# A two-layer hybrid trunk on one core: memory projected behind the second norm, stick breaking with queries and keys first, loads of constants and input moved

## The chip, the core and the metric

The kernel runs on one core of a Trainium2 chip. TensorE (PE) multiplies matrices, VectorE (DVE) and ScalarE (ACT) do elementwise work, GpSimd (POOL) only clears a few tiles, and SyncE (SP) issues every load and store. The metric is the device time of one execution in microseconds (us), lower is better. Before the change it is 1094.56 us, the median of 3 runs (1094.49 to 1095.02).

## The reference

The input is a sequence of 256 vectors of width 1024, in float32, with a fixed memory of 256 vectors. There are two layers; layer 0 mixes with an RWKV-7 recurrence, layer 1 with stick-breaking attention. Each layer is three residual blocks, each with a layer norm behind it:

```python
for i in range(DEPTH):                                   # DEPTH = 2
    x = layer_norm(ALPHA * x + 0.5 * swiglu(x, ffn1_w_gate[i], ffn1_w_up[i], ffn1_w_down[i]), ...)
    if i % 2 == 0:
        proj = x @ rwkv_w_in[0]                          # 2560 mixer columns, 256 memory queries
        mix = rwkv7_mix(proj[..., :RWKV_SHIFT], ...)
    else:
        proj = x @ sb_w_in[0]                            # q, k, v of 768 columns, 256 memory queries
        mix = stick_breaking_mix(...)
    heads = concatenate([mix, memory_attention(mq, mem_k, mem_v)], axis=-1)
    x = layer_norm(ALPHA * x + heads @ w_out[i], ...)
    x = layer_norm(ALPHA * x + 0.5 * swiglu(x, ffn2_w_gate[i], ffn2_w_up[i], ffn2_w_down[i]), ...)
```

The memory's keys and values, `mem @ w_mem_kv`, are computed once and used in both layers. The feed-forward width is 2816. In stick breaking the weight of a key is `exp(log_sigmoid(z) + later)`, where `later` is the sum of `-softplus(z)` over the keys between it and the query, so a softplus and a running sum stand between scores and output.

## The kernel before

The sequence is split into two halves of 128 rows, `hf` 0 and 1, each with its residual rows `xs[hf]` and their transpose `xT[hf]`. A float32 product with weights is made of three products of rounded parts (`mm3`, line 666): every weight piece of 512 KB is loaded to a `raw` tile, ScalarE rounds it to a `hi` tile, and VectorE subtracts to get the `lo` tile (`piece`, line 638). There are 10 raw, 9 hi and 9 lo buffers. A feed-forward network runs in 11 blocks of 256 columns (`ffn_block`, line 776): 8 steps of gate and up products into one bank of PSUM (tag `gu`), the activation, a transpose, and the down products into two accumulator banks of the half (`acc0` or `acc1`). A block listed in `WHOLE` (line 60) makes its down products in plain float32 from the raw weights, without hi and lo tiles. FFN intermediates sit in two buffers of tag `ta`, which other small tiles share.

The program lists operations in the order of the lines from 1448 on. For each layer it runs the first FFN with half 0 ahead of half 1, then `norm(0, ...)`; then the mixer of half 0, with the remaining FFN blocks of half 1 spread between its steps (`alternate`, line 1419); then `norm(1, ...)`; then the mixer of half 1 is opened, `mixed_out(0, ...)` multiplies half 0's heads with `w_out`, `norm(0, ...)` follows, and the second FFN's blocks of half 0 are spread between the steps of half 1's mixer. The dictionaries `RW` and `SB` (lines 50 and 51) say how many FFN steps go behind each named step of a mixer (`yield "nat"` and so on). `PRE[i]` is the number of steps of half 1's mixer that are listed before `mixed_out(0)`.

In layer 0 `memory_kv` (line 844) stands between `norm(0)` with one block of half 1 and the mixer of half 0. It loads the memory's rows, transposes them, multiplies them with four pieces of `w_mem_kv` and leaves `memKT` and `memV`. `mem_attention` (line 868) computes scores, softmax and values with them and writes the last two of the eight transposed pieces of the heads into `xT[hf]`; both mixers call it inside their own steps, with the accumulator banks of their half. `mixed_out` (line 1404) takes the four pieces of `w_out` in the order 3, 0, 1, 2; piece 3 belongs to the memory heads.

`stick` (line 1319) projects five times 512 columns: the last 256 columns of V with the memory queries, then q, q with k, k, the first 512 columns of V; then it does the memory attention, then the scores, softplus, running sums and outputs.

The listed order is not the order of issue. `Plan` (line 133) records all operations with their dependences and a price for each. `Plan.order` (line 348) then schedules them as a list scheduler with one clock for each engine; `Plan.latest` (line 499) computes from a schedule how late each operation may start; `Plan.improve` (line 544) makes 24 such schedules, with priorities from the latest starts, shaken at random from `SEED`, and keeps the one whose planned end is first. Loads go through SP's one queue in an order of their own (`nc.in_turn("load", ...)`): they are sorted by planned latest start, those in `lead` by the latest start of a named operation less 4 us. An SP load whose buffer is not free yet holds up all loads behind it.

Of the kernel before, what the change touches and what calls it, by code (L numbers as in the profile page):

```python
# [47 lines left out]
FIRST = 2  # L48
PRE = (0, 3)
RW = dict(p0=0, p1=0, p2=0, p3=0, p4=0, lb=0, sub=14, rb=0.5, kq=1, nat=0.5, dy=4, dt=2, c0=1.0, c1=1, c2=1.5, c3=2, t0=0, t1=10)  # L50
SB = dict(z0=3.0, z1=0, ln=2.0, e0=1.0, e1=1.5, o=6.0)
HOLD = (2, 4)
# [6 lines left out]
BESIDE = (True, False)  # L59
WHOLE = (((0, 1, 2, 3, 4, 5, 6, 8, 9, 10), (0, 1, 2, 4, 5, 6, 7, 8, 9)), ((), ()))  # L60


LINE = 16
BLK = 16
_LEVELS = [16, 32]
# [62 lines left out]
PATIENCE = 8  # L128
SEED = 144
TURN = 47040.0  # L130
# [474 lines left out]
def kernel(ctx, tc, const, x, mem, f1g, f1u, f1d, f2g, f2u, f2d, ln_g, ln_b, w_out, w_mem_kv,  # L605
# [168 lines left out]


    def ffn_block(w, c, halves, beside, whole):
        gv, uv, dv = (m.rearrange("(k p) c -> p k c", p=P) for m in w)
# [37 lines left out]
        o = {hf: ps("gu") for hf in halves}  # L815
        for k in range(KT):
            wh, wl = (t[:, k % 2] for t in gu[k // 2])
            for hf in halves:
                mm3(o[hf], xT[hf][0][:, k], xT[hf][1][:, k], wh, wl, k == 0, k == KT - 1)
            yield  # L820
        hs = {}
# [45 lines left out]

    def mem_attention(hf, mqT):

        rs = new(tp_, [P, 3, NMH], F32, "rs", "rs", 2)  # L870
        banks = [ps(f"acc{hf}").rearrange("p (j m) -> p j m", j=2) for p in range(2)]
        rows = [slice(p * HD, (p + 1) * HD) for p in range(2)]
# [5 lines left out]
        for p, scv in enumerate(banks):  # L878
# [16 lines left out]
            nc.copy(turned_e[-1], pt.rearrange("p (j m t) -> p j m t", j=2, m=2))  # L895
        o = ps(f"acc{hf}")
        ov = o[:, :MEMW].rearrange("p (j t) -> p j t", j=2)
# [7 lines left out]

    def sl(n, shape=None):
        return new(mp, shape or [P, MIX], F32, n, n)

# [16 lines left out]
    R = {}  # L925

    def rwkv_constants():
        vrow = new(tp_, [44, P], F32, "ta", "vrow", 2)
        for r0, n, src in ((0, 20, r_mu), (20, 6, r_a0), (26, 6, r_kk), (32, 6, r_ka)):
            nc.in_turn("load", nc.sync.dma_start(vrow[r0:r0 + n], src[0].rearrange("(a b) -> a b", b=P)))  # L930
        nc.in_turn("load", nc.sync.dma_start(vrow[38:44], r_rk[0].rearrange("(a c) b -> a (c b)", c=2)))
        gup = new(cp, [P, MIX], F32, "gup", "gup")
        nc.in_turn("load", nc.sync.dma_start(gup, r_gup[0]))
        vc = cp.tile([P, 44], F32, tag="vc", name="vc")
        pt = ps("tp")
        nc.tensor.transpose(pt[:, :44], vrow, ident[:44, :44])
        nc.copy(vc, pt[:, :44])
        for n, a, b in (("mu", 0, 20), ("a0", 20, 26), ("k_k", 26, 32), ("k_a", 32, 38), ("r_k", 38, 44)):
            R[n] = vc[:, a:b]
        rkb = cp.tile([P, NT, NH], F32, tag="rkb", name="rkb")  # L940
        nc.vector.tensor_tensor(rkb, hsel, bc(R["r_k"], 2, [P, NT, NH]), ALU.mult)
        S = new(cp, [P, NT, 2, HD], F32, "S", "S")
        nc.gpsimd.memset(S, 0.0)
        lastc = cp.tile([P, 20], F32, tag="lastc", name="lastc")
        nc.gpsimd.memset(lastc, 0.0)
        R.update(gup=gup, rkb=rkb, S=S, lastc=lastc)

    def rwkv(hf, res):
# [123 lines left out]
        shifted(1792, 512, lambda i: zv[:, 2 + i])  # L1072
        mem_attention(hf, mq)

# [244 lines left out]
    def stick(hf, res):  # L1319
# [7 lines left out]
        B[hf] = kT, V  # L1327
        t = project(hf, sb_in[0], 2048, 512)
        nc.copy(V[:, 512:768], t[:, 0:256])
        mq = new(mp, [P, 2, P], F32, "mq", "mq")  # L1330
        nc.copy(mq, turned(t, 2, 2), 0.125)
        yield "p"
        t = project(hf, sb_in[0], 0, 512)
# [9 lines left out]
        yield "p"  # L1343
        t = project(hf, sb_in[0], 1536, 512)
        nc.copy(V[:, 0:512], t)
        yield "p"
        mem_attention(hf, mq)
        zs, sps, first, logs = {}, {}, [], []
        v3 = lambda t: t.rearrange("q (i t) -> q i t", i=3)
        for si, ts in enumerate(range(hf, -1, -1)):  # L1350
            zm = zs[ts] = sl("qr" if si == 0 else "Sk", [P, 4, 384])
            sps[ts] = [sl(n, [P, 2, 384]) for n in (("L", "Lm") if si == 0 else ("T", "Tt"))]
            for jg in range(2):
# [15 lines left out]
                first.append(nc.scalar.activation(e, e, AF.Exp, scale=-1.0).i)  # L1369
                yield "z1"  # L1370
        for ts in zs:
            for jg in range(2):
                e, zz = sps[ts][jg], zs[ts][:, 2 * jg:2 * jg + 2]
                logs.append(nc.scalar.activation(e, e, AF.Ln, bias=1.0))
                logs[-1].after += first
                nc.vector.scalar_tensor_tensor(e, zz, 0.0, e, ALU.max, ALU.add)
            yield "ln"
        for ts in zs:
            for g in range(4):
                zm = zs[ts][:, g]  # L1380
                cu = ps("tp")
                nc.tensor.matmul(cu[:, :384], K_("tri"), sps[ts][g // 2][:, g % 2], start=True, stop=ts == hf)
                if ts != hf:
                    nc.tensor.matmul(cu[:, :384], K_("ones"), sps[hf][g // 2][:, g % 2], start=False, stop=True)
                nc.vector.tensor_sub(zm, zm, cu[:, :384])
                nc.scalar.activation(zm, zm, AF.Exp).after += [o.i for o in logs]
                yield "e0"
                yield "e1"
        tss = sorted(zs)
        for g in range(2):  # L1390
            o = ps(ac)
# [11 lines left out]

    def mixed_out(hf, y, w):
        t = xT[hf]
        if y is not None:
            to_T(y, t, 0, NT)
        open_acc(hf)
        for n in range(2):
            yield from cols_mm(acc[hf][n], t, cols_pieces(w, n * 512, 512, (3, 0, 1, 2)))  # L1410

# [104 lines left out]
```

## Time and profile before

| | us |
|---|---|
| median of 3 runs | 1094.56 |
| the profiled execution | 1096.41 |
| its span, first to last instruction | 1094.4 |
| TensorE busy | 1067.0 |
| VectorE busy | 895.0 |
| ScalarE busy | 719.9 |
| mean granted TensorE clock | 0.993 |

The span is what the trace covers; the profiled execution has some 2 us around it, and it is one run, slower than the median by 1.85 us. A line of the kernel says little here, because nearly all operations are recorded by one helper (line 601); tiles tell more. `xTh` and `xTl` are the transposed rows, `hi_`, `lo_` and `raw_` weights, `ps_29r` and `ps_30r` the two banks of `gu`, `ps_25r` to `ps_28r` the accumulators, `ps_2r` and `ps_3r` the banks for transposes and small products. The buffer of a tile keeps the name of its first user, so `h_31r` may hold constants, and `qr_404r` and `L_370r` hold scores and softplus in layer 1. A busy TensorE means that records of matmuls follow on one another; their ends are modelled.

### The profile page before, as it was taken

Reading aid. Unit: us, or ns where it says so; the run is one execution under the profiler, and the core shown is the slowest. Engines: PE = TensorE matmul, PEld = TensorE weight load, DVE = VectorE, ACT = ScalarE, POOL = GpSimd, SP = SyncE. Lnnn points to the kernel's source line nnn. Section 1 sums busy time; section 2 is a strip of 40 time slices with the busy share of each in tenths; the row PEclk is TensorE's granted clock in tenths of the full one; section 3 lists DMA queues with packets and bytes.
Section 4 is the critical chain, followed back from the end, with each engine's and each line's share of the span. In section 5 each row is a group of like instructions: output and inputs, shape, how many; then the busy total and the mean of one; then the engine's idle time right before and its main releaser. Section 6 shows DMA issues by size and latency. Waiting matters only on the chain.

```text
span 1094.4 us, 17466 instructions
## 1 busy us (share of the span) xinstructions
PE 1067.0 (97%) x6217; PEld 852.9 (78%) x6217; DVE 895.0 (82%) x1269; ACT 719.9 (66%) x991; POOL 2.7 (0%) x14
## 2 busy tenths in 40 slices
PE   7999999999799999999999999999989999999996
PEld 6878887877688777778888888888867777888885
DVE  6577676999999998787779965659799989987777
ACT  6466556966379684556657654538896899766652
POOL 0000000000000000000000000000000000000000
PEclk9999999999899999999999999999999999999999
DMA  9499768775778698699789976758978987999881
GB/s 335 160 356 386 255 221 286 260 246 193 247 230 285 232 295 274 210 329 336 254 273 365 307 262 204 229 159 287 382 270 293 340 301 239 396 358 316 249 292 59
DMA packets 209784, 300.13 MB, mean 274 GB/s; under 512 B 13684, under 2 KB 157216, under 8 KB 209698
## 3 DMA queue, kind: packets, MB, share of 16 engines
q1 hardware_dynamic: 209698, 299.03, 80.7%
q8 instruction: 48, 0.79, 0.3%
q14 instruction: 38, 0.31, 0.1%
HBM read 297.93 MB, written 1.05 MB: 273 GB/s over the span
## 4 chain that ended last, share of the span: by engine, by line
PE 90%; DVE 6%; DMA 2%; issue 1%; ACT 1%; SPq 0%; DVEq 0%; ACTq 0%
PE ps_30r L601 27%; PE ps_29r L601 27%; PE ps_28r L601 8%; PE ps_27r L601 8%; PE ps_25r L601 7%; PE ps_26r L601 7%; PE ps_2r L601 3%; PE ps_3r L601 3%; DVE x L601 1%; DMA raw_45r<-in_sb_w_in_dram 1%; DMA raw_21r<-in_ffn_w_up_dram 1%; DMA raw_9r<-in_ffn_w_up_dram 1%; DVE lb_475r L601 0%; DVE lo_8r L601 0%; DVE S_110r L601 0%
## 5 line engine op out<-in xcount | busy, mean ns | idle before, releaser
L601 ACT ACTIVATE h_31r<-ps_30r 128x256 f32<-128x256 f32 (+1 forms) x53 | 22.8, 430 | 33.6 <-PE ps_30r L601 33.6
L601 ACT ACTIVATE h_32r<-ps_29r 128x256 f32<-128x256 f32 (+1 forms) x53 | 22.0, 414 | 30.0 <-PE ps_29r L601 29.6
L601 PE MATMUL ps_29r<-hi_37r,xTh 128*128 128x512 f32 x58 | 24.2, 417 | 0.0
L601 PE MATMUL ps_29r<-hi_37r,xTl 128*128 128x512 f32 x58 | 22.7, 392 | 0.0
L601 PE MATMUL ps_29r<-lo_38r,xTh 128*128 128x512 f32 x58 | 22.6, 390 | 0.0
L601 PE MATMUL ps_30r<-hi_16r,xTh 128*128 128x512 f32 x54 | 22.6, 418 | 0.0
L601 PE MATMUL ps_29r<-hi_22r,xTh 128*128 128x512 f32 (+1 forms) x54 | 21.9, 406 | 0.0
L601 PE MATMUL ps_30r<-hi_10r,xTh 128*128 128x512 f32 x54 | 21.9, 405 | 0.0
L601 PE MATMUL ps_30r<-hi_40r,xTh 128*128 128x512 f32 x52 | 21.8, 420 | 0.0
L601 DVE TENSOR_TENSOR h_32r<-h_32r,ps_29r 128x256 f32<-128x256 f32 x32 | 13.4, 418 | 9.6 <-ACT h_32r L601 9.2
L601 PE MATMUL ps_30r<-hi_7r,xTh 128*128 128x512 f32 x50 | 21.2, 424 | 0.0
L601 PE MATMUL ps_30r<-hi_16r,xTl 128*128 128x512 f32 x54 | 21.2, 392 | 0.0
L601 PE MATMUL ps_30r<-lo_17r,xTh 128*128 128x512 f32 x54 | 21.1, 392 | 0.0
L601 PE MATMUL ps_30r<-lo_11r,xTh 128*128 128x512 f32 x54 | 21.1, 391 | 0.0
L601 PE MATMUL ps_30r<-hi_10r,xTl 128*128 128x512 f32 x54 | 21.1, 391 | 0.0
L601 PE MATMUL ps_29r<-lo_23r,xTh 128*128 128x512 f32 (+1 forms) x54 | 20.3, 376 | 0.8 <-DVE lo_23r L601 0.8
L601 PE MATMUL ps_29r<-hi_7r,xTh 128*128 128x512 f32 x50 | 20.9, 418 | 0.0
L601 PE MATMUL ps_30r<-hi_19r,xTh 128*128 128x512 f32 x50 | 20.8, 417 | 0.0
L601 PE MATMUL ps_30r<-hi_13r,xTh 128*128 128x512 f32 x50 | 20.6, 413 | 0.0
L601 PE MATMUL ps_29r<-lo_8r,xTh 128*128 128x512 f32 x50 | 20.2, 404 | 0.5 <-DVE lo_8r L601 0.5
L601 PE MATMUL ps_29r<-hi_10r,xTh 128*128 128x512 f32 x50 | 20.6, 411 | 0.0
L601 PE MATMUL ps_2r<-cst,x 128*128 128x128 f32 x48 | 8.8, 313 | 12.0 <-DVE x L601 6.5
(1909 smaller groups left out, 3958.0 us busy)
## 6 DMA issues: line engine op xcount, KB each, us to landing
raw_9r<-in_ffn_w_gate_dram SPq DMA_DIRECT2D x32, 256.0 KB, 5.4
raw_9r<-in_ffn_w_up_dram SPq DMA_DIRECT2D x32, 256.0 KB, 5.0
raw_18r<-in_ffn_w_down_dram SPq DMA_DIRECT2D x16, 512.0 KB, 4.8
raw_12r<-in_ffn_w_gate_dram SPq DMA_DIRECT2D x31, 256.0 KB, 5.8
raw_12r<-in_ffn_w_up_dram SPq DMA_DIRECT2D x31, 256.0 KB, 4.7
raw_24r<-in_ffn_w_down_dram SPq DMA_DIRECT2D x15, 512.0 KB, 6.1
raw_39r<-in_ffn_w_down_dram SPq DMA_DIRECT2D x15, 512.0 KB, 5.9
raw_42r<-in_ffn_w_down_dram SPq DMA_DIRECT2D x15, 512.0 KB, 6.0
```

The lines of the kernel that those rows point to most:

```text
L601: fn(*[at(x) for x in a], **{n: at(x) for n, x in k.items()})
```

## The change

1. `memory_kv` is taken from before half 0's mixer in layer 0 to behind `norm(1, ...)`. The mixer of half 0 in layer 0 no longer calls `mem_attention`; it hands its memory queries on, and the attention runs behind `memory_kv` with banks of tag `gu`. `mixed_out(0)` of layer 0 takes the pieces of `w_out` in the order 0, 1, 2, 3.
2. `stick` projects q and k first. V and the memory queries are projected behind the scores, and the memory attention follows them.
3. The constants' loads get a fixed early place in SP's queue. The second half's input is loaded and transposed in the first FFN block that needs it, whose gate and up products go half by half; each half's input is loaded in two pieces.
4. Numbers of the plan: `PRE`, `RW`, `SB`, `WHOLE` and `SEED`. Names that are new and switched off (`PARTED` empty, `LATE` false) change nothing.

```diff
-PRE = (0, 3)
-RW = dict(p0=0, p1=0, p2=0, p3=0, p4=0, lb=0, sub=14, rb=0.5, kq=1, nat=0.5, dy=4, dt=2, c0=1.0, c1=1, c2=1.5, c3=2, t0=0, t1=10)
-SB = dict(z0=3.0, z1=0, ln=2.0, e0=1.0, e1=1.5, o=6.0)
+PRE = (0, 0)
+RW = dict(p0=0, p1=0, p2=0, p3=0, p4=0.5, lb=0, sub=14, rb=0.5, kq=1, nat=10, dy=4, dt=1.5, c0=1.0, c1=1, c2=6, c3=2, t0=0, t1=10)
+SB = dict(z0=3.0, z1=0, ln=2.0, e0=1.0, e1=1.5, o=12)
-WHOLE = (((0, 1, 2, 3, 4, 5, 6, 8, 9, 10), (0, 1, 2, 4, 5, 6, 7, 8, 9)), ((), ()))
+WHOLE = (((0, 1, 2, 3, 4, 5, 6, 8, 9, 10), (0, 1, 2, 4, 5, 6, 7, 9)), ((3,), ()))
+MEMTAG = 'gu'
+PARTED = ()
+LATE = False
+XPARTS = 2
+ORDERS = ((0, 1, 2, 3), (3, 0, 1, 2), (1, 0, 3, 2), (3, 0, 1, 2))
-SEED = 144
+SEED = 8617
+    def load_x(hf):
+        xs[hf] = xp.tile([P, D], F32, tag=f"x{hf}", name=nm("x"))
+        for n in range(XPARTS):
+            sl = slice(n * D // XPARTS, (n + 1) * D // XPARTS)
+            nc.in_turn("load", nc.sync.dma_start(xs[hf][:, sl], x[0, half_sl(hf), sl]))
+        turn_x(hf)
...
-        for k in range(KT):
-            wh, wl = (t[:, k % 2] for t in gu[k // 2])
-            for hf in halves:
-                mm3(o[hf], xT[hf][0][:, k], xT[hf][1][:, k], wh, wl, k == 0, k == KT - 1)
-            yield
+        apart = [[hf] for hf in halves] if None in xs else [halves]
+        for group in apart:
+            if xs[group[0]] is None:
+                load_x(group[0])
+            for k in range(KT):
+                wh, wl = (t[:, k % 2] for t in gu[k // 2])
+                for hf in group:
+                    mm3(o[hf], xT[hf][0][:, k], xT[hf][1][:, k], wh, wl, k == 0, k == KT - 1)
+                yield
...
+    def early(o):
+        nc.in_turn("load", o)
+        nc.lead[o.i] = EARLY[0]
+    EARLY = [0]
...
         shifted(1792, 512, lambda i: zv[:, 2 + i])
-        mem_attention(hf, mq)
+        if hf == 0:
+            res.append(mq)
+        else:
+            mem_attention(hf, mq)
...
-        t = project(hf, sb_in[0], 2048, 512)
-        nc.copy(V[:, 512:768], t[:, 0:256])
-        mq = new(mp, [P, 2, P], F32, "mq", "mq")
-        nc.copy(mq, turned(t, 2, 2), 0.125)
-        yield "p"
         t = project(hf, sb_in[0], 0, 512)
...
-        t = project(hf, sb_in[0], 1536, 512)
-        nc.copy(V[:, 0:512], t)
-        yield "p"
-        mem_attention(hf, mq)
...
                 yield "z1"
+        t = project(hf, sb_in[0], 2048, 512)
+        nc.copy(V[:, 512:768], t[:, 0:256])
+        mq = new(mp, [P, 2, P], F32, "mq", "mq")
+        nc.copy(mq, turned(t, 2, 2), 0.125)
+        yield "p"
+        t = project(hf, sb_in[0], 1536, 512)
+        nc.copy(V[:, 0:512], t)
+        yield "p"
+        if not LATE:
+            mem_attention(hf, mq)
...
-    for hf in range(NHALF):
-        xs[hf] = xp.tile([P, D], F32, tag=f"x{hf}", name=nm("x"))
-        nc.in_turn("load", nc.sync.dma_start(xs[hf], x[0, half_sl(hf), :]))
-        turn_x(hf)
+    load_x(0)
...
             run(blocks(w, seq[:2]))
-            nc.in_turn("load", nc.sync.dma_start(cst[:, P:], const[:, P:]))
+            EARLY[0] = len(nc.ops) - 1
+            early(nc.sync.dma_start(cst[:, P:], const[:, P:]))
             run(blocks(w, seq[2:4]))
             rwkv_constants()
...
         run(blocks(w, solo(1, range(HEAD)), BESIDE[0], WHOLE[i][0]))
-        if i == 0:
-            run(memory_kv())
         alternate(chain_steps(mixer(0, mixed)), blocks(w, solo(1, range(HEAD, lag1)), True, WHOLE[i][0]), steps)
         norm(1, 2.0 * ALPHA, 4.0 * LN_EPS, gb)
...
         for _ in range(PRE[i]):
             next(second)
-        run(chain_steps(mixed_out(0, mixed[0], w_out[i])))
+        if i == 0:
+            run(memory_kv())
+            mem_attention(0, mixed.pop(0), MEMTAG)
+        run(chain_steps(mixed_out(0, mixed[0], w_out[i], i)))
```

All loads of constants in `rwkv_constants` use `early` in place of `nc.in_turn`. In the running sums of `stick` the one or two products of a bank are bound together.

More of the change, by code (lines that the diff above doesn't have):

```diff
@@ L866, in memory_kv, with mem_attention @@
             nc.copy(memKT[:, :, half_sl(hf)], pt[:, :2 * P].rearrange("p (j t) -> p j t", t=P))
-    def mem_attention(hf, mqT):
+    def mem_attention(hf, mqT, tag=None):
+        tag = tag or f"acc{hf}"
         rs = new(tp_, [P, 3, NMH], F32, "rs", "rs", 2)
-        banks = [ps(f"acc{hf}").rearrange("p (j m) -> p j m", j=2) for p in range(2)]
+        banks = [ps(tag).rearrange("p (j m) -> p j m", j=2) for p in range(2)]
         rows = [slice(p * HD, (p + 1) * HD) for p in range(2)]
@@ L895, in mem_attention @@
             nc.copy(turned_e[-1], pt.rearrange("p (j m t) -> p j m t", j=2, m=2))
-        o = ps(f"acc{hf}")
+        o = ps(tag)
         ov = o[:, :MEMW].rearrange("p (j t) -> p j t", j=2)
@@ L904, in mem_attention, with sl @@
         split_T(o, xT[hf], NT, 2)
-    def sl(n, shape=None):
-        return new(mp, shape or [P, MIX], F32, n, n)
+    def sl(n, shape=None, dtype=F32):
+        return new(mp, shape or [P, MIX], dtype, n, n)
     def project(hf, w, c0, n):
@@ L929, in rwkv_constants @@
         for r0, n, src in ((0, 20, r_mu), (20, 6, r_a0), (26, 6, r_kk), (32, 6, r_ka)):
-            nc.in_turn("load", nc.sync.dma_start(vrow[r0:r0 + n], src[0].rearrange("(a b) -> a b", b=P)))
-        nc.in_turn("load", nc.sync.dma_start(vrow[38:44], r_rk[0].rearrange("(a c) b -> a (c b)", c=2)))
+            early(nc.sync.dma_start(vrow[r0:r0 + n], src[0].rearrange("(a b) -> a b", b=P)))
+        early(nc.sync.dma_start(vrow[38:44], r_rk[0].rearrange("(a c) b -> a (c b)", c=2)))
         gup = new(cp, [P, MIX], F32, "gup", "gup")
-        nc.in_turn("load", nc.sync.dma_start(gup, r_gup[0]))
+        early(nc.sync.dma_start(gup, r_gup[0]))
         vc = cp.tile([P, 44], F32, tag="vc", name="vc")
@@ L1343, in stick @@
         yield "p"
-        t = project(hf, sb_in[0], 1536, 512)
-        nc.copy(V[:, 0:512], t)
-        yield "p"
-        mem_attention(hf, mq)
-        zs, sps, first, logs = {}, {}, [], []
+        zs, sps, parts, first, logs = {}, {}, {}, [], []
+        tri = {F32: (K_("tri"), K_("ones"))}
+        if hf in PARTED:
+            t = new(cp, [P, 2, P], F32R, "tri", "tri")
+            nc.copy(t, cst[:, _WHERE["tri"][0]:_WHERE["ones"][1]].rearrange("p (a b) -> p a b", a=2))
+            tri[F32R] = t[:, 0], t[:, 1]
         v3 = lambda t: t.rearrange("q (i t) -> q i t", i=3)
@@ L1376, in stick @@
                 nc.vector.scalar_tensor_tensor(e, zz, 0.0, e, ALU.max, ALU.add)
+                parts[ts, jg] = (e,)
+                if hf in PARTED and ts == hf:
+                    parts[ts, jg] = hi, lo = [sl(n, [P, 2, 384], F32R) for n in (("RB", "Y"), ("g", "lb"))[jg]]
+                    nc.copy(hi, e)
+                    nc.vector.tensor_sub(lo, e, hi.bitcast(F32))
             yield "ln"
@@ L1381, in stick @@
                 cu = ps("tp")
-                nc.tensor.matmul(cu[:, :384], K_("tri"), sps[ts][g // 2][:, g % 2], start=True, stop=ts == hf)
+                sums = [(tri[x.dtype][0], x[:, g % 2]) for x in parts[ts, g // 2]]
                 if ts != hf:
-                    nc.tensor.matmul(cu[:, :384], K_("ones"), sps[hf][g // 2][:, g % 2], start=False, stop=True)
+                    sums += [(tri[x.dtype][1], x[:, g % 2]) for x in parts[hf, g // 2]]
+                with nc.together():
+                    for n, (m, x) in enumerate(sums):
+                        nc.tensor.matmul(cu[:, :384], m, x, start=n == 0, stop=n == len(sums) - 1)
                 nc.vector.tensor_sub(zm, zm, cu[:, :384])
@@ L1389, in stick @@
         tss = sorted(zs)
+        if LATE:
+            mem_attention(hf, mq)
         for g in range(2):
@@ L1402, in stick, with mixed_out @@
         res.append(None)
-    def mixed_out(hf, y, w):
+    def mixed_out(hf, y, w, last=3):
         t = xT[hf]
@@ L1409, in mixed_out @@
         for n in range(2):
-            yield from cols_mm(acc[hf][n], t, cols_pieces(w, n * 512, 512, (3, 0, 1, 2)))
+            yield from cols_mm(acc[hf][n], t, cols_pieces(w, n * 512, 512, ORDERS[last]))
     def run(*gens):
```

## The prediction

> **What bounds the kernel now.** I read the page's busy line and its chain first, then who TensorE (PE) waits for, then a table of stretches cut where the waits lie.
>
> ```profile
> PE 1067.0 (97%) x6217; PEld 852.9 (78%) x6217; DVE 895.0 (82%) x1269; ACT 719.9 (66%) x991; POOL 2.7 (0%) x14
> PE 90%; DVE 6%; DMA 2%; issue 1%; ACT 1%; SPq 0%; DVEq 0%; ACTq 0%
> ```
> ```profile
> PE ps_2r L601 <- DVE x L601: 6.5, 2, 5.8
> PE ps_2r L601 <- DMA x<-in_x_dram: 4.9, 1, 4.9
> PE ps_2r L601 <- DVE L_370r L601: 1.7, 1, 1.7
> PE ps_3r L601 <- DVE x L601: 1.3, 2, 0.8
> PE ps_2r L601 <- DVE qr_404r L601: 1.1, 1, 1.1
> PE ps_29r L601 <- DVE lo_23r L601: 0.8, 1, 0.8
> PE ps_25r L601 <- DVE lo_44r L601: 0.7, 1, 0.7
> ```
> ```profile
> 61.00:66.00 5.00, 3.56 (x15) 2.26 (x14) 2.91 (x4) 2.91 (x3) 0.00 (x0) 1.00 1.08 379
> 165.00:185.00 20.00, 19.96 (x91) 15.22 (x90) 11.34 (x13) 10.06 (x16) 0.00 (x0) 1.00 0.84 271
> 185.00:286.00 101.00, 100.68 (x1008) 77.03 (x1008) 95.86 (x172) 73.40 (x126) 0.20 (x1) 1.00 0.71 239
> 286.00:292.60 6.60, 6.58 (x152) 6.16 (x148) 6.42 (x14) 3.01 (x5) 0.64 (x3) 1.00 0.90 345
> 292.60:298.40 5.80, 0.04 (x1) 0.04 (x1) 5.63 (x23) 0.00 (x0) 0.00 (x0) 0.64 0.86 247
> 298.40:304.50 6.10, 6.10 (x20) 5.13 (x21) 6.02 (x14) 2.25 (x3) 0.00 (x0) 0.50 0.32 88
> 400.00:450.00 50.00, 50.00 (x651) 36.95 (x649) 42.15 (x71) 27.27 (x42) 0.00 (x0) 1.00 0.77 254
> 816.00:827.00 11.00, 6.99 (x43) 3.90 (x42) 10.86 (x25) 9.28 (x14) 0.00 (x0) 1.00 0.41 140
> 860.00:865.00 5.00, 4.18 (x21) 3.25 (x20) 5.00 (x10) 3.49 (x5) 0.00 (x0) 1.00 0.85 284
> 1083.00:1094.40 11.40, 2.40 (x11) 1.60 (x9) 6.95 (x17) 0.00 (x0) 0.00 (x0) 0.79 0.12 46
> ```
>
> In the table, after the stretch and its length, come the busy us of PE, weight load, DVE, ACT and POOL, then the granted clock and the DMA. PE is the bound: 1094.4 − 1067.0 leaves 27.4 us in which it has nothing. Of these 4.9 wait for the input and 11.40 − 2.40 = 9.0 are the last norm, which the change leaves alone. The rest lies in three places that it does touch: 5.8 us at 292.6, where DVE is busy 5.63 of 5.80 with the second norm of layer 0; 4.0 us at 816 to 827 and 0.8 at 860 (layer 1); 1.44 us at 61 to 66.
>
> The first hole costs more than its length. After it the clock is 0.50 for 6.10 us:
>
> ```profile
> 300.32 2.56 PE ps_25r L601 x6
> 307.11 4.08 PE ps_25r L601 x18
> ```
>
> These are rows of the chain: 2.56 / 6 = 0.43 us a matmul there, 4.08 / 18 = 0.227 later. Half of 6.10, 3.05 us, is lost too, so the hole is worth 5.8 + 3.05 = 8.85 us.
>
> **The memory block (layer 0).** memory_kv moves from before rwkv(0) to behind norm(1), with the memory attention of half 0. What moves on PE: 2 x 24 matmuls of 0.227 = 10.9, 20 transposes, and the attention:
>
> ```profile
> 165.09 0.60 PE L601 MATMUL ps_3r<-cst,raw_21r 128*128 128x128 f32 x4
> 231.16 0.48 PE L601 MATMUL ps_25r<-memKT,mq_353r 64*128 64x256 f32 x1
> 240.33 0.27 PE L601 MATMUL ps_25r<-pT_352r,memV 128*64 128x128 f32 x1
> 166.59 1.22 DVE L601 TENSOR_TENSOR lo_17r<-raw_48r,hi_16r 128x1024 fp32r<-128x1024 f32 x1
> 167.72 0.69 DVE L601 TENSOR_TENSOR lo_11r<-ps_3r,hi_10r 128x512 fp32r<-128x512 f32 x1
> 232.32 0.69 DVE L601 TENSOR_REDUCE rs_457r<-ps_25r 128x2 f32<-128x512 f32 x1 [0.16 <-PE ps_26r L601]
> ```
>
> Transposes: 0.60 / 4 = 0.15 at most, so 20 are 3.0 or less; I take 2.2. The attention runs 0.9 us for its scores (four pairs some 0.21 apart), as much for the products with memV and for 8 transposes: 2.6. Together 15.7 us of PE work, against a hole of 5.8: enough cover. ACT's part, the high halves and the exponentials, finds it busy 3.01 of 6.60 us at 286 and idle after. On DVE move 4 x 1.22 + 4 x 0.69 = 7.6, and with the attention (two reductions of 0.69, its split of some 0.4, small ones) 2.1 more: 9.7 us. Four w_mem_kv pieces and two memory rows, 6 x 512 KB, leave SP's queue ahead of rwkv(0)'s weights and go into it again before the second norm. At the 345 GB/s of the row at 286 they take 9.1 us, which the 0.71 DMA share at 185 to 286 can hide if they are issued early; issued late they wait at a DMA share of 0.90.
>
> What hides it: PE has this work while DVE ends norm(1). What is late next: y of rwkv(0) and its projection. The w_out pieces of the memory columns go last there, so the attention ends the row; its 2.1 us of DVE stand on that path. I take 8.85 − 2.1 = **6.75 us gained**. Bounds: 8.85 if DVE keeps up, and a loss of 6.85 (second rival).
>
> Can rwkv(0) do without the cover? Between 165 and 298.4 DVE is busy 11.34 + 95.86 + 6.42 + 5.63 = 119.3 of 133.4 us. With the idle share of 185 to 286 (5.14 of 101) everywhere, 119.3 us of work take 125.7: 7.7 us less than now, and 5.8 are needed. That is why I go near the upper end: the 8.7 idle DVE us at 165 to 185, where PE does the memory instead of rwkv(0)'s projections, are what the change can use.
>
> [...]
>
> **Stick breaking (layer 1).** q and k come first, then z, then mq and V, then the memory attention. The output's steps get 12 FFN steps each instead of 6, and PRE 3 becomes 0. The hole by its rows:
>
> ```profile
> 818.02 0.91 PE L601 MATMUL ps_2r<-L_370r,cst 128*128 128x384 f32 x2 [1.65 <-DVE L_370r L601]
> 820.71 0.91 PE L601 MATMUL ps_2r<-Lm_355r,cst 128*128 128x384 f32 x2 [1.13 <-DVE qr_404r L601]
> 824.22 0.66 PE L601 MATMUL ps_2r<-cst,x 128*128 128x128 f32 x4 [0.76 <-DVE x L601]
> 825.35 0.66 PE L601 MATMUL ps_3r<-cst,x 128*128 128x128 f32 x4 [0.47 <-DVE x L601]
> 864.41 0.63 PE L601 MATMUL ps_3r<-cst,x 128*128 128x128 f32 x4 [0.82 <-DVE x L601]
> ```
>
> The FFN filler of half 1 is used up at 816 while softplus, running sums and norm(1) all go over DVE. Two projections (48 x 0.227 = 10.9 us) that lay ahead of the scores can now lie behind them: more cover than 4.0 + 0.8. DVE stays full there (10.86 of 11.00), so I leave the two norm waits of 0.76 and 0.47 standing and count 4.83 − 1.23 = **3.6 gained**; bounds 0 and 4.83. The `together` in the running sums changes no work, since PARTED is empty; the new step counts of RW (nat 10, c2 6) only share out the same filler, whose worst case is the second rival.
>
> WHOLE puts FFN block 3 of half 1 in layer 1 to fp32 down products (the dropped 8 is never run there: half 0 has blocks 0 to 7). Four fp32 products in place of twelve:
>
> ```profile
> 467.37 1.72 PE ps_26r L601 x4
> ```
>
> Each fp32 product makes two of these records, 2 x 0.43 = 0.86 us; 4 x 0.86 − 12 x 0.227 = **0.72 lost** on PE, while DVE loses two pieces of 1.22 and a split. Both ends are close, so it is counted in full.
>
> **Constants and input.** A stretch by its busy times, then SP's queue and PE's waits:
>
> ```profile
> 36.00:53.00 17.00, 17.00 (x80) 13.97 (x78) 7.70 (x9) 5.67 (x8) 0.00 (x0) 1.00 0.16 56
> 34.72 0.37 SPq L601 DMA_DIRECT2D raw_12r<-in_ffn_w_up_dram  x1
> 53.14 0.31 SPq L601 DMA_DIRECT2D h_31r<-in_rwkv_mu_dram  x1
> 63.10 0.50 PE L601 MATMUL ps_25r<-lo_44r,hT_35r 128*128 128x512 f32 x1 [0.68 <-DVE lo_44r L601]
> 65.56 0.50 PE L601 MATMUL ps_29r<-lo_23r,xTh 128*128 128x512 f32 x1 [0.76 <-DVE lo_23r L601]
> ```
>
> For 18 us nothing leaves the queue: the constants wait for a buffer that holds an FFN intermediate, and the weights wait behind them. PE pays 0.68 + 0.76. With the constants set 4 us ahead of the end of the second block, the five small loads, gup and the constant array come sooner: **1.4 gained**; bounds 0 and 1.44. They still wait for such a buffer, and all weights queued behind them wait too, but the pause now begins with fuller buffers ahead of PE.
>
> The second half's 512 KB go behind the first weights, and each half comes in two pieces (one issue more per half). PE's first block waits for that load between its halves; behind it on SP stand the next blocks' weights.
>
> ```profile
> 10.57 0.79 PE L601 MATMUL ps_29r<-lo_8r,xTh 128*128 128x512 f32 x1 [0.47 <-DVE lo_8r L601]
> 10.00:14.40 4.40, 3.93 (x10) 3.06 (x10) 4.40 (x6) 4.12 (x5) 0.00 (x0) 1.00 1.05 404
> ```
>
> At 404 GB/s the weights come 1.3 us sooner. But ten matmuls in 4.40 us is the half rate again, so 1.3 us sooner is 0.65 us of work, and the 8 transposes of half 1, now hidden under the first load, cost up to 8 x 0.15 = 1.2. I count **0**; bounds −1.3 and +1.2.
>
> **Sum.** −6.75 − 3.6 + 0.72 − 1.4 = −11.0 us. The profiled execution took 1096.41 us (span 1094.4 and 2.0 around it): 1085.4. The median of the runs shown, 1094.56, is 1.85 lower than that, so 1083.5. With my bounds on the single terms the forecast itself reaches from 1079 (all holes closed: −8.85 − 4.83 + 0.72 − 1.44 − 1.3 = −15.7) to 1088.
>
> **Rivals.**
> 1. The hole only moves. If the 9.7 us of DVE work push norm(1) back as far as the cover reaches, layer 0 gains 0 and the rest stays: 1094.56 − 3.6 + 0.72 − 1.4 = 1090.3. For it: DVE 95.86 of 101.00. Against: the 8.7 idle DVE us at 165 to 185.
> 2. Slower: rwkv(0) starves PE. If its chain doesn't start earlier, the 15.7 us of PE work taken out turn to idle time inside 165 to 286, and the memory behind gives only 8.85 back: +6.85, with the rest −4.3, so 1097.1. The point: the chain must move up by 6.9 us (15.7 − 8.85); below it layer 0 loses. For it: PE and DVE are both full at 185 to 286. Against: the projections that wait at 165 to 185.
> 3. No change: every queue order is planned anew (another seed), so holes of the same sum can open elsewhere: about 1094.5.
> 4. More is gained. In 400 to 450 PE is "busy" throughout, yet weight loads fill 36.95, against 0.82 of the time (13.97 of 17.00 at 36 to 53), 41 of 50, where large matmuls run without a break: some 4 to 5 us of hidden waits. If the new plan takes those too: 1078.5. [...]
>
> **Numbers.** Forecast 0.64, rivals in order 0.12, 0.11, 0.06, 0.07. Faster by over 0.2% (below 1092.4; 0.2% is about what a measurement of this kernel can tell): 0.64 + 0.12 + 0.07 = 0.83; slower 0.11; same 0.06. The range 1077.5 to 1092.5 holds the faster cases.
>
> **What would show it.** Right: no PE wait for x near 290, clock 1.00 there, memory matmuls in that place, and PE full at 160 to 290; no waits for L and qr near 816; SP's queue without an 18 us pause. Wrong: PE waits for DVE inside rwkv(0), or below-full clock there; memory weights landing late behind norm(1).

## The result, and the profile after

The changed kernel takes 1085.66 us (median of 4 runs, 1083.32 to 1086.21) against 1094.53 us for the kernel before on the same chip: a ratio of 0.9918, 95% interval 0.9903 to 0.9932. Its profiled execution took 1085.55 us with a span of 1083.5. The forecast was 1083.5 us with a range of 1077.5 to 1092.5.

The same views as before, of the changed kernel. The busy line and the shares of the chain:

```profile
PE 1063.7 (98%) x6213; PEld 848.4 (78%) x6213; DVE 890.6 (82%) x1267; ACT 721.0 (67%) x990; POOL 2.7 (0%) x14
PE 94%; DVE 4%; DMA 1%; ACT 0%; issue 0%; SPq 0%; DVEq 0%; ACTq 0%
```

PE's waits (total, times, longest). The names of the banks have moved: `ps_22r` to `ps_25r` are now the accumulators, `ps_26r` and `ps_27r` the two banks of `gu`.

```profile
PE ps_2r L606 <- DMA x<-in_x_dram: 4.4, 1, 4.4
PE ps_26r L606 <- ACT hi_4r L606: 2.8, 1, 2.8
PE ps_2r L606 <- DVE xTl L606: 1.1, 1, 1.1
PE ps_2r L606 <- ACT memKT L606: 0.6, 1, 0.6
PE ps_27r L606 <- DVE xTl L606: 0.5, 1, 0.5
```

The table of stretches (start and end, length, busy us of PE, weight load, DVE, ACT, POOL, then clock, DMA share, GB/s), with the cuts of before, and the two wide stretches of layers 0 and 1:

```profile
36.00:53.00 17.00, 17.00 (x77) 14.04 (x76) 12.29 (x14) 10.94 (x14) 0.00 (x0) 1.00 1.05 371
165.00:185.00 20.00, 20.00 (x92) 15.12 (x90) 18.04 (x25) 15.54 (x24) 0.00 (x0) 1.00 1.03 369
286.00:292.60 6.60, 4.88 (x31) 3.33 (x29) 6.60 (x13) 5.86 (x11) 0.00 (x0) 1.00 0.73 188
298.40:304.50 6.10, 6.10 (x39) 4.73 (x38) 6.01 (x9) 4.90 (x8) 0.00 (x0) 1.00 0.97 344
816.00:827.00 11.00, 11.00 (x55) 9.10 (x54) 10.78 (x22) 7.97 (x8) 0.00 (x0) 1.00 0.93 313
400.00:450.00 50.00, 50.00 (x660) 38.44 (x660) 41.29 (x68) 28.66 (x42) 0.00 (x0) 1.00 0.75 245
240.00:310.00 70.00, 67.93 (x784) 53.00 (x783) 63.14 (x117) 43.64 (x74) 0.64 (x3) 1.00 0.77 256
780.00:840.00 60.00, 59.45 (x290) 45.12 (x289) 55.77 (x86) 48.90 (x70) 0.00 (x0) 1.00 0.82 278
840.00:900.00 60.00, 59.76 (x316) 46.68 (x315) 53.26 (x64) 57.12 (x85) 0.00 (x0) 1.00 0.87 318
```

The last three stretches of the kernel before:

```profile
240.00:310.00 70.00, 63.90 (x867) 49.10 (x864) 65.73 (x130) 37.97 (x66) 0.64 (x3) 0.93 0.67 222
780.00:840.00 60.00, 55.99 (x294) 43.15 (x294) 54.31 (x78) 52.04 (x75) 0.00 (x0) 1.00 0.82 287
840.00:900.00 60.00, 59.18 (x319) 47.17 (x318) 53.05 (x70) 51.03 (x76) 0.00 (x0) 1.00 0.95 333
```

Layer 0's stretch had 6.1 us of idle PE and 10.2 us at half clock (0.93 is its mean); now 2.07 us are idle and the clock stays at 1.00. Layer 1's two stretches go from 4.83 us idle to 0.79. At 36 to 53 the DMA moves 371 GB/s where it moved 56.

Idle time alone misses matmuls that run slowly (0.43 us apart behind the hole of the kernel before, 0.227 later) or lie further apart than usual while PE counts as busy. So I also took all PE rows of a trace, summed the distances from one matmul's start to the next, and subtracted for each the usual shortest distance of its shape at full clock (0.227 us for a rounded product of 512 columns). What is left over is **time beyond work**; half-clock time counts in it.

| us | before | after | difference |
|---|---|---|---|
| first matmul, and beyond work to 20 | 4.92 + 5.6 | 4.43 + 6.3 | +0.2 |
| 20 to 100 (constants) | 3.0 | 1.0 | −2.0 |
| 240 to 310 (layer 0) | 15.4 | 9.8 | −5.6 |
| 560 to 780 | 2.2 | 3.1 | +0.9 |
| 780 to 900 (layer 1) | 12.0 | 6.7 | −5.3 |
| work itself (WHOLE) | 1026.2 | 1026.9 | +0.7 |

These add up to −11.1; the two profiled executions differ by 10.86. The cuts stay at the same times while the work moves up, by as much as 13 us in layer 0, and the usual distance of the small products is a choice, so a row is good to a microsecond or two. With the median distance of each shape and kind of tile as the usual one (products that run side by side left out), 240 to 310 gains 7.2, of which 100 to 240 gives 2.4 back; 780 to 900 gains 4.4 and the time behind it 1.9. Either way layer 0 is worth some 5 us and layer 1 some 5 to 6.

### The profile page after: what moved, and what is told of

The parts are those of the page before. It is cut to its first block, busy times and chain, and to the rows that moved or that the text cites. A ratio compares the mean times of both kernels' runs of the same rounds, so it can differ in the third digit from the quotient of the medians.

```text
span 1083.5 us, 17483 instructions
## 1 busy us (share of the span) xinstructions
PE 1063.7 (98%) x6213; PEld 848.4 (78%) x6213; DVE 890.6 (82%) x1267; ACT 721.0 (67%) x990; POOL 2.7 (0%) x14
## 4 chain that ended last, share of the span: by engine, by line
PE 94%; DVE 4%; DMA 1%; ACT 0%; issue 0%; SPq 0%; DVEq 0%; ACTq 0%
PE ps_27r L606 27%; PE ps_26r L606 27%; PE ps_25r L606 8%; PE ps_24r L606 8%; PE ps_22r L606 8%; PE ps_23r L606 8%; PE ps_3r L606 4%; PE ps_2r L606 4%; DMA raw_42r<-in_ffn_w_down_dram 1%; DVE x L606 1%; DMA raw_6r<-in_ffn_w_up_dram 0%; DVE Y_337r L606 0%; DVE xTl L606 0%; SPq L606 0%; DVE lo_5r L606 0%
## 5 line engine op out<-in xcount | busy, mean ns | idle before, releaser
L606 PE MATMUL ps_26r<-hi_4r,xTh 128*128 128x512 f32 x54 | 22.5, 416 | 2.8 <-ACT hi_4r L606 2.8
L606 PE MATMUL ps_27r<-hi_19r,xTh 128*128 128x512 f32 x56 | 23.7, 423 | 0.0
L606 PE MATMUL ps_27r<-hi_43r,xTh 128*128 128x512 f32 x54 | 22.2, 411 | 0.0
L606 PE MATMUL ps_26r<-lo_5r,xTh 128*128 128x512 f32 x54 | 21.7, 402 | 0.5 <-DVE lo_5r L606 0.5
L606 PE MATMUL ps_27r<-hi_7r,xTh 128*128 128x512 f32 x54 | 22.1, 410 | 0.0
L606 PE MATMUL ps_27r<-hi_16r,xTh 128*128 128x512 f32 x52 | 22.1, 425 | 0.0
L606 PE MATMUL ps_27r<-hi_19r,xTl 128*128 128x512 f32 x56 | 21.9, 391 | 0.0
L606 PE MATMUL ps_27r<-lo_20r,xTh 128*128 128x512 f32 x56 | 21.9, 391 | 0.0
L606 PE MATMUL ps_27r<-hi_4r,xTh 128*128 128x512 f32 x54 | 21.7, 402 | 0.0
L606 PE MATMUL ps_26r<-hi_4r,xTl 128*128 128x512 f32 x54 | 21.6, 400 | 0.0
```

Of the source, the lines that this page charges most:

```text
L606: fn(*[at(x) for x in a], **{n: at(x) for n, x in k.items()})
```

## The experiments

Each row compares with runs of the kernel before on the same chip. Its median differs between the chips by up to 1 us (1094.5 to 1095.5), so rows are best compared by their ratios.

| kernel | median us (runs) | ratio to before, 95% interval |
|---|---|---|
| after | 1085.66 (4) | 0.9918, 0.9903 to 0.9932 |
| before, new seed | 1098.38 (10) | 1.0030, 1.0021 to 1.0040 |
| after, old seed | 1085.56 (4) | 0.9911, 0.9888 to 0.9935 |
| after, memory as before | 1090.80 (5) | 0.9960, 0.9944 to 0.9977 |
| before, memory moved | 1091.23 (10) | 0.9965, 0.9954 to 0.9975 |
| before, hole filled | 1093.80 (11) | 0.9992, 0.9983 to 1.0000 |
| after, old order in stick | 1084.48 (4) | 0.9908, 0.9895 to 0.9922 |
| before, new order in stick | 1104.46 (4) | 1.0091, 1.0078 to 1.0105 |
| after, constants as before | 1087.75 (4) | 0.9939, 0.9923 to 0.9954 |
| before, new counts in layer 1 | 1093.64 (11) | 0.9984, 0.9975 to 0.9993 |
| after, old counts in layer 1 | 1092.68 (9) | 0.9977, 0.9967 to 0.9986 |
| after, input as before | 1083.61 (4) | 0.9898, 0.9885 to 0.9912 |
| after, old order and old input | 1083.88 (4) | 0.9901, 0.9885 to 0.9918 |

**The plan's seed.** The third rival said that a plan drawn anew opens holes of its own. First the kernel before with the new seed:

```diff
-SEED = 144
+SEED = 8617
```

> The kernel before with the plan's seed of after, nothing else. Theory (the parts of the change close the holes, the seed only redraws the order): 1092.5 to 1096.5 us; TensorE still waits some 5 us for x at the second norm of layer 0 and the granted clock is at half for some 10 us behind it. Rival (the new plan is what gained): near 1086, holes gone.

Then the changed kernel with the old one:

```diff
-SEED = 8617
+SEED = 144
```

> The kernel after with the seed of before, nothing else. Theory: 1084 to 1088 us, no wait for x near 290 and full clock there. Rival (the plan gained): near 1094, a hole of some 5 us somewhere in layer 0 or 1.

The seed alone costs the kernel before 0.3%, more than the theory allowed (1098.38 against 1092.5 to 1096.5). Its waits show how (y of rwkv(0) in layer 0, then a norm's statistics in layer 1):

```profile
PE ps_26r L601 <- DVE Y_365r L601: 5.1, 1, 5.1
PE ps_2r L601 <- DVE mv_608r L601: 3.0, 1, 3.0
```

With the old seed the changed kernel keeps its gain (0.9911), though the clock isn't full near 290 as was expected (0.98 over 240 to 310). So the gain doesn't hang on the seed. But each edit below, the filled hole aside, also draws the plan anew, and the seed shows that this alone can move a kernel by 3.7 us. A difference of that size counts only where the traces show it in its place.

**The memory block.** Undone in the changed kernel, with its order of the `w_out` pieces:

```diff
-        if hf == 0:
-            res.append(mq)
-        else:
-            mem_attention(hf, mq)
+        mem_attention(hf, mq)
...
+        if i == 0:
+            run(memory_kv())
         alternate(chain_steps(mixer(0, mixed)), ...
...
-        if i == 0:
-            run(memory_kv())
-            mem_attention(0, mixed.pop(0), MEMTAG)
```

> After with memory projection, memory attention of half 0 and the order of the output weights in layer 0 as before. Theory: the hole at the second norm of layer 0 is back with the half clock behind it, 5.6 us by the stretch 240 to 310 of the two traces and up to 8.85 by the hole itself: 1091 to 1094.5 us. Rival (the other parts or the seed closed it): 1085 to 1088, no such hole.

The reverse, put alone into the kernel before:

> Before with the memory part alone (projection behind the second norm, attention of half 0 behind it, output weights in the order 0 to 3 in layer 0). Theory: the hole of 5.8 us and the half clock go, the layer 1 hole of 4.0 stays: 1086 to 1090 us. Rival (the memory work only starves the first mixer, and the gain needs the other step counts too): 1093 to 1097, new waits between 160 and 290.

Undone it costs 1090.80 − 1085.66 = 5.1 us by the medians and 4.6 by the ratios, just below the expected band; alone it gains 0.35%, 3.8 us, a little short of the expected. First the wait and the stretch of the changed kernel without it, then two stretches of the kernel before with it:

```profile
PE ps_22r L606 <- DVE Y_365r L606: 3.8, 1, 3.8
```
```profile
240.00:310.00 70.00, 64.00 (x853) 48.62 (x845) 65.71 (x128) 38.72 (x65) 0.64 (x3) 0.98 0.66 224
```
```profile
240.00:310.00 70.00, 67.43 (x780) 52.26 (x779) 63.55 (x114) 43.80 (x75) 0.64 (x3) 1.00 0.76 258
780.00:840.00 60.00, 57.17 (x290) 43.83 (x287) 55.24 (x80) 50.70 (x73) 0.00 (x0) 0.94 0.83 288
```

Without the memory in that place PE is idle 6.0 us of the 70, though its longest wait is now for y of rwkv(0) and not for x, and the clock is hardly slowed (0.98, where the kernel before has 0.93). With the memory there it is idle 2.57, and layer 1 still has its hole (2.83 idle, clock 0.94). The part acts by itself and in its own place. The new counts of `RW` were in the one kernel and not in the other; no run undoes them alone.

That rwkv(0) doesn't starve is shown by the moments of its output statistics and of the second norm's x, before and after:

```profile
293.95 1.00 DVE L601 TENSOR_REDUCE hs_602r<-L_370r 128x6 f32<-128x384 f32 x2
297.55 1.41 DVE L601 SCALAR_TENSOR_TENSOR x<-x,mv_608r,raw_42r 128x512 f32<-128x512 f32 x2
```
```profile
280.40 1.01 DVE L606 TENSOR_REDUCE hs_564r<-L_342r 128x6 f32<-128x384 f32 x2
285.97 0.74 DVE L606 SCALAR_TENSOR_TENSOR x<-x,mv_570r,raw_6r 128x512 f32<-128x512 f32 x1
290.79 1.21 DVE L606 TENSOR_TENSOR lo_20r<-raw_42r,hi_19r 128x1024 fp32r<-128x1024 f32 x1
291.92 0.68 DVE L606 TENSOR_TENSOR xTl<-ps_2r,xTh 128x512 fp32r<-128x512 f32 x1
```

The chain ends 13.55 us sooner, with 6.9 as the point below which the second rival would have come true. With the memory put back into the changed kernel the same statistics stand at 292.96, so 12.56 us of this are the memory's move. The room came from 165 to 185, where DVE is now busy 18.04 of 20 us (11.34 before, and 11.04 with the memory put back). Of the 2.07 us that stay idle, 1.08 are for the bank `ps_2r`, out of which DVE still has to take the low part of x (`xTl` at 291.92), behind a subtraction for weights (`lo_20r`); 0.61 are for the same bank, out of which ScalarE copies `memKT`; and 0.28 are for the low part of y. DVE is full there (6.60 of 6.60 at 286 to 292.6).

**What the half clock costs.** Half of 6.10 us was a term of mine. This kernel keeps the plan of before and puts six products whose results nobody reads into the hole, so that only the clock changes:

```diff
             for _, _, o in order:
+                if o.i == self.mark[0]:
+                    c = self.mark[1]
+                    for n in range(6):
+                        bank = real[("ps", "gu"), n % 2]
+                        self.real.tensor.matmul(bank[:, :512], c[:, :128], c[:, 128:640], start=True, stop=True)
```

> Before, its plan untouched, with six float32 matmuls (128x512, some 0.86 us each) whose results nobody reads put on TensorE in the hole at 292.6 to 298.4 us. They do no work for the output. Theory (an idle hole costs its length and the half clock behind it): the wait for x shrinks to about 0.7 us, the clock is 1.00 at 298 to 305 and the time falls by 3.05 us: 1091 to 1092. Rival (the half clock is covered by other work or only in the records): 1094 to 1095, no change.

The stretch behind the hole in the filled kernel, and then PE's timeline (start, busy us), from the first transposes of x to the first product behind the transposes of y, in the kernel before and in the filled one:

```profile
298.40:304.50 6.10, 5.45 (x28) 3.83 (x28) 6.03 (x15) 3.04 (x5) 0.00 (x0) 1.00 0.33 91
```
```profile
298.36 1.11 PE L601 MATMUL ps_2r<-cst,x 128*128 128x128 f32 x4 [5.78 <-DVE x L601]
304.56 0.48 PE L601 MATMUL ps_26r<-hi_7r,xTh 128*128 128x512 f32 x1
```
```profile
298.91 0.65 PE L606 MATMUL ps_2r<-cst,x 128*128 128x128 f32 x4 [0.43 <-DVE x L606]
302.78 0.80 PE L606 MATMUL ps_2r<-cst,Y_365r 128*128 128x128 f32 x4 [0.20 <-DVE Y_365r L606]
303.33 0.48 PE L606 MATMUL ps_26r<-hi_7r,xTh 128*128 128x512 f32 x1
```

The clock does stay at 1.00, and the filling delays nothing, since PE still waits 0.43 us for x behind it. The same work takes 303.33 − 298.91 = 4.42 us in place of 304.56 − 298.36 = 6.20: 1.78 us gained on the spot, and 0.9 (0 to 1.9) in the time, not 3.05. DVE is busy 6.03 of 6.10 us with the fast clock as with the slow one (6.02), and PE now waits for y.

**Order of the projections in stick breaking.** My step credited the new order with closing layer 1's hole. Undone in the changed kernel (the two blocks go back ahead of q and k):

```diff
+        t = project(hf, sb_in[0], 2048, 512)
...
         t = project(hf, sb_in[0], 0, 512)
...
+        t = project(hf, sb_in[0], 1536, 512)
...
+        mem_attention(hf, mq)
         zs, sps, parts, first, logs = {}, {}, {}, [], []
...
-        t = project(hf, sb_in[0], 2048, 512)
...
-        t = project(hf, sb_in[0], 1536, 512)
```

> After with the projections of stick breaking in the order of before (V's end and memory queries first, then q, k, V, then the memory attention, then scores); step counts, seed and all else as after. Theory: waits for x, softplus and running sums of some 4 to 5 us come back near 815, so 1089 to 1091.5 us. Rival (the step counts and PRE closed the hole): 1085 to 1087.

And alone, in the kernel before:

> Before with the order of projections in stick breaking of after alone (step counts and PRE as before). Theory: the hole of 4.0 at 816 and 0.8 at 860 shrink by 3 to 5 us: 1089.5 to 1092. Rival (the order alone does nothing): 1093.5 to 1095.5, waits for L and qr as before.

Both went against the theory. Without the new order the changed kernel takes 1084.48 us, no longer than with it, and 780 to 900 loses 7.2 us beyond work (6.7 with it). The new order alone costs the kernel before 9.7 us. PE is idle 5.47 us at 780 to 900 (4.83 before), now mostly for ScalarE at the tile of the scores, and the clock falls to 0.94 in both stretches:

```profile
PE ps_26r L601 <- ACT qr_404r L601: 3.4, 2, 3.0
```
```profile
780.00:840.00 60.00, 56.53 (x285) 43.56 (x284) 51.98 (x76) 52.34 (x75) 0.00 (x0) 0.94 0.76 266
840.00:900.00 60.00, 58.00 (x284) 46.94 (x283) 57.06 (x72) 51.31 (x66) 0.00 (x0) 0.94 0.96 338
```

Part of the 9.7 us lies in layer 0, which the edit doesn't touch: PE is idle 7.98 us at 240 to 310 there (6.10 before), which I put down to the redrawn plan.

**Step counts in layer 1.** The theory formed then: the counts, PRE 0 in place of 3 and 12 FFN steps behind an output step, let `mixed_out(0)` go ahead of half 1's projections and lie under norm(1). Alone in the kernel before:

```diff
-PRE = (0, 3)
+PRE = (0, 0)
-SB = dict(z0=3.0, z1=0, ln=2.0, e0=1.0, e1=1.5, o=6.0)
+SB = dict(z0=3.0, z1=0, ln=2.0, e0=1.0, e1=1.5, o=12)
```

> Before, with only the step counts of layer 1 new (no step of half 1's mixer listed ahead of mixed_out of half 0, and 12 FFN steps instead of 6 behind each output step of half 0); the order of projections, the memory, the loads and the seed stay. Theory (the counts close the hole: half 0's output product, listed first, fills it): 780 to 900, which loses 12.0 us of PE time in before, loses 4 to 5 less, and the time falls to 1089 to 1091.5. Rival (the counts do it only together with the new order of projections): 1093.5 to 1096, with PE still waiting for softplus and running sums near 818.

The same lines turned round, in the changed kernel:

> After, with the step counts of layer 1 as they were before (three steps of half 1's mixer listed ahead of half 0's output product, 6 FFN steps behind an output step); the new order of projections stays. Theory (the counts are what made room, and the new order alone costs time): the waits of the kernel with the new order alone come back, 780 to 900 loses 12 to 17 us, and the time is 1091 to 1096. Rival (order and counts don't matter in the new plan): 1085 to 1086.5.

The stretches of the kernel before with the new counts, then the longest wait in layer 1 and the stretches of the changed kernel with the old ones:

```profile
780.00:840.00 60.00, 58.26 (x304) 45.22 (x303) 54.81 (x85) 51.45 (x74) 0.00 (x0) 1.00 0.83 285
840.00:900.00 60.00, 59.69 (x321) 47.34 (x320) 54.50 (x68) 54.49 (x83) 0.00 (x0) 1.00 0.97 348
```
```profile
PE ps_3r L606 <- DVE x L606: 4.1, 1, 4.1
```
```profile
780.00:840.00 60.00, 55.65 (x273) 41.89 (x273) 52.62 (x71) 48.47 (x70) 0.00 (x0) 0.97 0.83 281
840.00:900.00 60.00, 58.29 (x300) 46.16 (x299) 52.63 (x73) 54.89 (x78) 0.00 (x0) 1.00 0.87 299
```

Undoing the counts brings a hole back (6.06 us idle), now with a wait for x and not for the tile of the scores, and loses most of the gain: 0.9977 against 0.9918, 6.5 us. Putting them alone into the kernel before takes its 4.83 idle us to 2.05, and beyond work from 12.0 to 9.0, but the time only by 0.16%, 1.8 us: less than the theory said, and a time that the rival named, though its waits for softplus and running sums are gone. So the counts are what the changed kernel needs, and only together with the rest are they worth that much. The old order of projections suffers less from old counts (1094.5) than the new order does (1104.5, or 1092.7 in the changed kernel); with new counts the order makes no difference beyond the scatter.

Two things stay open. The 6.5 us hold what the new order costs under old counts, and the run that would take this out, the changed kernel with old order and old counts, was not made. With the old order, the new counts take the loss at 780 to 900 from 12.0 to 9.0 in the kernel before, and it is 7.2 in the changed kernel: 3 to 5 us. And `PRE` and the 12 steps were only changed together; which of them does it wasn't measured.

The mechanism, in the first rows of DVE's timeline that take an accumulator of half 1 and of half 0 into x, for the changed kernel with the old counts and then as it is; behind them the first and the last row of a run of products in PE's timeline of the changed kernel:

```profile
808.61 0.68 DVE L606 SCALAR_TENSOR_TENSOR x<-x,ps_24r 128x512 f32<-128x512 f32 x1
841.23 0.68 DVE L606 SCALAR_TENSOR_TENSOR x<-x,ps_22r 128x512 f32<-128x512 f32 x1
```
```profile
812.62 0.69 DVE L606 SCALAR_TENSOR_TENSOR x<-x,ps_25r 128x512 f32<-128x512 f32 x1 [0.19 <-PE ps_25r L606]
821.79 0.68 DVE L606 SCALAR_TENSOR_TENSOR x<-x,ps_23r 128x512 f32<-128x512 f32 x1
```
```profile
815.03 0.50 PE L606 MATMUL ps_23r<-hi_43r,xTh 128*128 128x512 f32 x1
...
825.18 0.39 PE L606 MATMUL ps_22r<-hi_19r,xTl 128*128 128x512 f32 x1
```

norm(1) begins at 808.61 and 812.62. With the old counts half 0's output product is taken into norm(0) 33 us later; as it is, 9 us later. Its products into `ps_23r` and `ps_22r` follow on one another, 0.23 us apart, through the time of norm(1), in which PE waits 4.1 us for x with the old counts.

**Constants.** Changed kernel without the early place:

```diff
-        nc.lead[o.i] = EARLY[0]
```

> After without the fixed early place of the constants in SP's queue (they are sorted by their own latest start, as before); all else as after. Theory: SP's queue stands still for some 18 us before 55 us again, TensorE waits about 1.5 us for lo tiles near 63 us, so 1087 to 1088. Rival (the input's move keeps the queue full enough): 1085 to 1086, no such wait.

```profile
20.00:100.00 80.00, 78.01 (x347) 62.75 (x346) 53.98 (x60) 46.63 (x61) 0.00 (x0) 1.00 0.82 290
36.00:53.00 17.00, 17.00 (x78) 14.03 (x77) 9.02 (x11) 7.42 (x10) 0.00 (x0) 1.00 0.26 92
```

2.1 us by the medians, as expected: the queue pauses again (92 GB/s at 36 to 53) and PE is idle 1.99 us of 80, where the changed kernel has no idle time.

**Input.**

```diff
-XPARTS = 2
+XPARTS = 1
...
     load_x(0)
+    load_x(1)
```

> After, with the input loaded as before: both halves up front, each in one piece. My count was 0, with bounds of -1.3 and +1.2 for the new way. Theory (the weights don't come sooner, and the second half's eight transposes now stand in PE's way): the first 20 us lose 0.5 to 1 less and the time is 1084.5 to 1085.5. Rival (the split start pays): 1086.5 to 1087.

The median, 1083.61, is lower than expected, but the intervals of the two ratios overlap, and the traces don't place the gain in the start. What they show, changed kernel first, then with the input as before:

```profile
4.43 1.09 PE L606 MATMUL ps_2r<-cst,x 128*128 128x128 f32 x4 [4.43 <-DMA x<-in_x_dram]
9.17 0.80 PE L606 MATMUL ps_26r<-hi_4r,xTh 128*128 128x512 f32 x1 [2.80 <-ACT hi_4r L606]
13.08 0.40 PE L606 MATMUL ps_26r<-lo_8r,xTh 128*128 128x512 f32 x1
```
```profile
4.90 1.08 PE L606 MATMUL ps_2r<-cst,x 128*128 128x128 f32 x4 [4.90 <-DMA x<-in_x_dram]
9.77 0.79 PE L606 MATMUL ps_29r<-hi_7r,xTh 128*128 128x512 f32 x1 [0.40 <-ACT hi_7r L606]
15.46 0.63 PE L606 MATMUL ps_30r<-hi_7r,xTl 128*128 128x512 f32 x1
```

The first weight product starts at 9.17 against 9.31 in the kernel before and 9.77 here: taking 512 KB from ahead of the weights didn't bring them the 1.3 us that I had worked out as one bound. One pair of traces says little here: the first weight product starts at 8.06 to 9.17 us in the six kernels with the split input and at 9.01 to 9.77 in the eight with whole pieces, 0.7 sooner on average, and in the eight the second half's transposes stand ahead of it on PE. The likely reason for so little is the rate: from 4 to 8 us the DMA moves 276 GB/s in the changed kernel and 361 in the kernel before, where my bound reckoned with 404 throughout. Why it is slower behind the split input wasn't settled. And the comparison is disturbed by PE's rate: a product of 512 columns lasts 0.40 from 13.08 on in the one execution and still 0.63 at 15.46 in the other. Whether the split start costs up to 2 us or nothing stays open.

**Both undone.** The last kernel leaves out the two parts that didn't show a gain by themselves, the order of projections and the split input.

> After, with two parts undone that didn't pay by themselves: the order of projections in stick breaking (V and memory queries first, as before) and the input loaded up front in one piece for each half. Memory, constants and step counts stay as in after. Theory (the two gains of 1.2 and 2 us are real and independent): a ratio to before of 0.987 to 0.989. Rival (each lay within the scatter of its runs, or the new plan gives them back): 0.990 to 0.992, that of after.

0.9901, the rival's side. The two small gains don't add up; the changed kernel, it with the old seed, the old order, the old input, and this one all lie at 0.9898 to 0.9918, with intervals that overlap. No version was found that is shown to beat the changed kernel.

## Why the prediction was right, and where it was not

- **What bounds the kernel**: right. Nearly all of the gain is PE time in or just around the three places named; the busy time of DVE hardly moved (895.0 to 890.6).
- **Memory block, 6.75 us**: mechanism right, size too high. 5.6 us by the traces, 4.6 to 5.1 by undoing it, 3.8 alone. I priced the half clock at half its length (3.05); filling the hole showed 1.78 on the spot. With 1.78 in place of 3.05 the sum is 5.8 + 1.78 − 2.1 = 5.5. That the 2.1 us which I took off for the attention's DVE part equal the 2.07 that stay idle is luck: PE waits there for a bank that DVE empties behind a subtraction for weights (1.08) and for the same bank behind ScalarE (0.61); only the 0.28 stand behind a reduction of the attention (`rs_602r`, 292.52).
- **Stick breaking, 3.6 us for the order of projections**: the wrong part of the change got the credit. "Two projections that lay ahead of the scores can now lie behind them" was not what filled the hole. The step counts, which I passed over in half a sentence, were: without them the changed kernel loses 6.5 us (3 to 5 are the counts' own, as far as the runs tell), without the order nothing. The two norm waits that I left standing (1.23) went too, so the traces show 5.3.
- **WHOLE, +0.72**: the rows of PE give +0.7 of work. No run undoes it alone. Its block stands at 810.6 to 814.1 us, right ahead of norm(1) of layer 1, and spares DVE two subtractions of 1.22 and a split there, so it may have a share in closing layer 1's hole that I didn't count.
- **Constants, −1.4**: −2.0 by the traces, 2.1 by undoing them. 1.44 is the idle time alone; beyond work PE lost 3.0 there.
- **Input, 0**: +0.2 by the traces, within the bounds; the weights' products came 0.1 us sooner in this pair of traces, and 0.7 on average over all of them, not 1.3.
- **The sum and the last step**: −11.0 was forecast between profiled executions, and they differ by 10.86 (1085.55 against my 1085.4). The 2.2 us by which the median misses 1083.5 come mostly from the step "that is 1.85 lower, so 1083.5": I carried the distance of one profiled execution from its median over to the other kernel, and the new profiled execution lies on its median (1085.55 and 1085.66). Between medians the change is worth 8.87. That a sum with one term too high and two too low came within 0.2 us of the profiled executions' difference is partly luck.
- **Rivals**: the hole only moves (1090.3) didn't happen: the chain moved up 13.55 us. rwkv(0) starved (1097.1) fell by the same number. A new plan alone gives +0.3%, and the changed kernel keeps its gain with the old seed, so the seed is no explanation. The hidden waits at 400 to 450 stayed: weight loads fill 38.44 of 50 us (36.95 before), time beyond work 7.7 (7.5).

## What to carry to other kernels

Where a list scheduler works from a written order, numbers that only say how many filler steps go where can be worth more than the reordering that stands beside them in the diff: ask of each which large piece of work it lets go ahead. Price an idle stretch by its length, and the slow clock behind it by what the next engine lets PE do there, not by half of the stretch (here 1.78 us, not 3.05). Where each edit makes the scheduler draw its plan anew, run the old kernel with another seed before an edit is credited with a few microseconds. Take a forecast from median to median, and treat one profiled execution's distance from its median as scatter (1.85 us in the kernel before, 0.11 in the changed one).

## What the runs showed of the hardware

- The half clock behind the hole cost less than half of its length. 10.2 us at 0.50 were taken away in the filled kernel: 4.2 of them lay in the hole itself, and the 6.1 behind it gave 1.78 us (4.42 in place of 6.20 for the same work), where half of 6.1, the forecast's estimate, is 3.05. At the full clock PE is busy 5.45 of these 6.10 us, and it waits 0.20 for y.
- Half-clock stretches in the middle of these traces differ in length: 10.2 us in the kernel before (0.50 from 294.2 to 304.4). With 0.50 as the lower clock in the others too, their mean clocks give, as estimates, 7.0 us in the kernel before with the memory moved (0.86 over 805 to 830) and 3.5 in the changed kernel with the old counts (0.84 over 816 to 827). What sets the lengths wasn't measured.
- The moment from which products run at full rate at the start varies between executions that start with the same work (products of 512 columns then last 0.39 in place of 0.63): about 14.5 us in the kernel before, about 9 in the one with new counts in layer 1. Time beyond work to 20 us is 5.6 in the one and 3.7 in the other. A start is to be compared with that in mind, and by the durations: the clock column reads 1.00 for 10.00 to 14.40 in the kernel before, where products follow 0.43 us apart.
- Less data ahead in a queue brought what follows less than its size says: with 512 KB fewer ahead, which would take 1.3 us at the 404 GB/s of 10 to 14.4 us, the first weight product started 0.7 us sooner on average (8.06 to 9.17 in six traces, 9.01 to 9.77 in eight), while from 4 to 8 us the DMA moved 276 GB/s in the changed kernel and 361 in the kernel before.
